# Row sums of attention's squares, five attention units later in TensorE's order

## The chip, the cores and the metric

The kernel runs on one NeuronCore of a Trainium2 chip. Its engines are named as in the profile: PE (TensorE, matrix multiplication; PEld is its weight load), DVE (VectorE), ACT (ScalarE), POOL (GpSimd) and SP (SyncE, which issues DMAs). Each engine executes its own queue in order, and waits on semaphores for the others. The metric is the device time of one execution in microseconds (us), lower is better.

## The reference

One decoder layer on 2048 tokens of width 1024, in float32. A normalised input is projected once; the columns go to two groups of heads, whose outputs are normalised, put side by side and projected again. A SwiGLU feed-forward part and a gated per-layer embedding follow.

```python
u = rmsnorm(h, attn_pre_norm[i])
proj = u @ w_in[i]
hq, hf, hi, hg, sq, sk, sv = jnp.split(proj, splits, axis=-1)
o_hg = hgrn2_mix(hq, hf, hi, lb_all[i])                        # 4 heads, gated linear recurrence
o_hg = rmsnorm(o_hg.astype(x.dtype), hg_out_norm[i]) * jax.nn.silu(hg)
o_sb = stick_breaking_mix(sq.reshape(B, T, SB_HEADS, SB_DH), ...)  # 8 heads of width 64, causal
o_sb = rmsnorm(o_sb, sb_out_norm[i])
mix = jnp.concatenate([o_hg, o_sb], axis=-1) @ w_out[i]
h = h + rmsnorm(mix, attn_post_norm[i])
u = rmsnorm(h, ffn_pre_norm[i])
gate, up = jnp.split(u @ w_gate_up[i], [D_FF], axis=-1)
y = (jax.nn.silu(gate) * up) @ w_down[i]
h = h + rmsnorm(y, ffn_post_norm[i])
h = h + (p[i] @ ple_proj[i]) * jax.nn.sigmoid(h @ ple_gate[i])
```

The line that matters here is `o_sb = rmsnorm(o_sb, ...)`: it needs, for each token, the sum of the squares of all 512 attention outputs.

## The kernel before

The 2048 tokens are four groups (0 to 3) of 512. A float32 product is made of three: each operand is split into a high part (ACT casts it, "wh", "uh", "ah") and a low part (DVE or POOL subtracts, "wl", "ul", "al"), and `mm3`, lines 216 to 218, multiplies high by high and the two mixed pairs. Weights come by DMA into one of four "wr" buffers and are split in `weight` (L202 on ACT, L203 on DVE and POOL in turn).

Attention is a stream of units (`attention`, L404). For a group g, a head h and a chunk c of 512 keys, a unit is one block of 128: `weights_of` makes the scores on PE (two matmuls into "z", L429), two sigmoids on ACT (L435, L436), a scan on DVE (L450) and the weights "a" on POOL (L454). Four units later (LAG), `turn_of` transposes the blocks of "a" on PE into the bank "tr" (L462, up to four transposes), ACT copies it out as the high part "ah" (L465) and DVE subtracts the low part "al" (L467). One unit later still, `values_of` multiplies both parts by the values into the bank "av" (L478 and L479). PSUM has eight banks: three "mm", two "z", and one each of "av", "tr" and "hg".

When a head is through, ACT and DVE bring its result to SBUF (L486, L487). After every second head, ACT squares the pair's result (L490), POOL adds the square to the tile "sbacc" (L492), and `result` splits it (L291 on ACT, L292 on DVE) and stores it (L293, L294). After the last head of a group four matmuls by a column of ones sum the squares over the partitions into four columns of "tr" (L497; in float32 each shows as two passes), and ACT copies them to "oss" (L498). The output projection of that group scales by them: POOL makes "rg" of "oss" (L655, L656).

The order of PE is the order in which the program is written (`manual_schedule` for PE alone); the other engines' orders are made by a scheduler from the dependencies and its own estimates, so they follow when PE's order changes. What PE does between the units comes from `weave`: it steps a main stream (an input projection of a group; after the last of these the output projections of groups 0 and 1) and the side streams (attention, HGRN2, operands of later stages) in a fixed rhythm. So attention of groups 0 to 2 ends in the middle of a projection, with the next group's units right behind, and that of group 3 ends with the output projection of group 1, "the second output projection". The third one (group 2) follows at once. HGRN2 has its own row sums (L639) in the bank "hg".

Of the kernel before, what the change touches and what calls it, by code (L numbers as in the profile page):

```python
# [8 lines left out]
F32 = mybir.dt.float32  # L9
# [6 lines left out]
P = 128  # L16
# [3 lines left out]
GT = 512  # L20
NG = T // GT
TT = GT // P
HH = 4
SBH = 8
# [66 lines left out]
def hybrid_block(  # L91
# [6 lines left out]
    nc = tc.nc  # L98
# [44 lines left out]
    ones1 = ctile("ones1", (P, 1))  # L143
# [15 lines left out]
    oss = ctile("oss", (P, NG, 2 * TT))  # L159
# [6 lines left out]
    def bank(tag):  # L166
        return ps.tile([P, 512], F32, tag=tag, name=tag, bufs=BANKS[tag])
# [19 lines left out]
    att = side.enter_context(tc.tile_pool(name="att", bufs=2, side="right"))  # L187
# [213 lines left out]
                yield  # L401


    def attention():  # L404
        def head_start(g, h):
            st = {"g": g, "h": h}
            st["q"] = []
            for i in range(2):
                t = att.tile([P, GT], F32R, tag=f"q{i}", name=f"q{i}")
                for half in range(2):  # L410
                    nc.sync.dma_start(t[half * SBD:(half + 1) * SBD, :].bitcast(F32), q_s[g][i, h])
                st["q"].append(t)
            return st

        def chunk_start(st, c):
            h = st["h"]
            kt = att.tile([P, GT], F32R, tag="kt", name="kt", bufs=2)
            nc.sync.dma_start(kt.bitcast(F32), k_s[c][h].rearrange("i d t -> (i d) t"))
            vt = att.tile([P, TT, P], F32R, tag="vt", name="vt", bufs=2)
            nc.sync.dma_start(vt.bitcast(F32), v_s[c][:, h, :].rearrange("(b s) d -> s b d", s=P))  # L420
            return {"st": st, "c": c, "k": kt, "v": vt, "a": []}

        def weights_of(ch, tb):
            st, c = ch["st"], ch["c"]
            diag = c == st["g"]
            n = (tb + 1) * P if diag else GT
            z = bank("z")
            for i in range(2):
                nc.tensor.matmul(  # L429
                    z[:, :n], st["q"][i][:, tb * P:(tb + 1) * P], ch["k"][:, :n],  # L430
                    start=i == 0, stop=i == 1)
            if diag:
                nc.vector.tensor_tensor(z[:, n - P:n], z[:, n - P:n], maskneg, op=ALU.add)  # L433
            be = att.tile([P, GT], F32, tag="be", name="be")
            nc.scalar.activation(be[:, :n], z[:, :n], AF.Sigmoid, scale=0.125)  # L435
            nc.scalar.activation(z[:, :n], z[:, :n], AF.Sigmoid, scale=-0.125)  # L436


            r, j = ring[tb], st["g"] - c
            o = GT if j % 2 == 0 else 0  # L440
            if diag:
                init = 1.0
                if c > 1:
                    nc.gpsimd.memset(r[:, o + n:o + n + 1], 1.0)
            elif j % 2 == 0:
                init = r[:, 0:1]
                nc.scalar.copy(r[:, 2 * GT:2 * GT + 1], init)
            else:
                init = r[:, GT:GT + 1]
            nc.vector.tensor_tensor_scan(  # L450
                r[:, o:o + n][:, ::-1], z[:, :n][:, ::-1], be[:, :n][:, ::-1], init,
                op0=ALU.mult, op1=ALU.bypass)
            a = att.tile([P, GT], F32, tag="a", name="a", bufs=8)
            nc.gpsimd.tensor_tensor(a[:, :n], be[:, :n], r[:, o + 1:o + n + 1], op=ALU.mult)  # L454
            ch["a"].append(a)

        def turn_of(ch, sb):
            diag = ch["c"] == ch["st"]["g"]
            t0 = sb if diag else 0
            tr = bank("tr")  # L460
            for tb in range(t0, TT):
                nc.tensor.transpose(tr[:, tb * P:(tb + 1) * P], ch["a"][tb][:, sb * P:(sb + 1) * P], ident)  # L462
            lo_c = t0 * P
            hi = att.tile([P, GT], F32R, tag="ah", name="ah")
            nc.scalar.copy(hi[:, lo_c:], tr[:, lo_c:])  # L465
            lo = att.tile([P, GT], F32R, tag="al", name="al")
            nc.vector.tensor_tensor(lo[:, lo_c:], tr[:, lo_c:], hi[:, lo_c:].bitcast(F32), op=ALU.subtract)  # L467
            return ch, sb, lo_c, hi, lo

        def values_of(ch, sb, lo_c, hi, lo):  # L470
            st, c = ch["st"], ch["c"]
            g = st["g"]
            first = c == g and sb == 0
            last = c == 0 and sb == TT - 1
            if first:
                st["av"] = bank("av")
            av = st["av"]
            nc.tensor.matmul(av[:, lo_c:], ch["v"][:, sb, :], hi[:, lo_c:], start=first, stop=False)  # L478
            nc.tensor.matmul(av[:, lo_c:], ch["v"][:, sb, :], lo[:, lo_c:], start=False, stop=last)  # L479
            if last:  # L480
                h = st["h"]
                mine, other = slice(h % 2 * SBD, (h % 2 + 1) * SBD), slice((1 - h % 2) * SBD, (2 - h % 2) * SBD)
                if h % 2 == 0:
                    avo[0] = att.tile([P, GT], F32, tag="avo", name="avo", bufs=1)
                o = avo[0]
                nc.scalar.copy(o[mine, :], av[other, :])  # L486
                nc.vector.tensor_tensor(o[mine, :], av[mine, :], o[mine, :], op=ALU.add)  # L487
                if h % 2:
                    sq = sb_acc if h == 1 else att.tile([P, GT], F32, tag="be", name="sq")
                    nc.scalar.activation(sq, o, AF.Square)  # L490
                    if h > 1:
                        nc.gpsimd.tensor_tensor(sb_acc, sb_acc, sq, op=ALU.add)  # L492
                    result(g, HH + h // 2, o, g_sb[:, h // 2:h // 2 + 1], nc.vector)
                    if h == SBH - 1:
                        b = bank("tr")
                        for t in range(TT):
                            nc.tensor.matmul(b[:, t:t + 1], sb_acc[:, t * P:(t + 1) * P], ones1, start=True, stop=True)  # L497
                        nc.scalar.copy(oss[:, g, TT:], b[:, 0:TT])  # L498

        sb_acc = att.tile([P, GT], F32, tag="sbacc", name="sbacc", bufs=1)  # L500
        avo = [None]
        units, turned = [], []
        chunks = [(g, h, c) for g in range(NG) for h in range(SBH) for c in range(g, -1, -1)]
        n_units = len(chunks) * TT
        for i in range(n_units + LAG + 1):
            if i < n_units:
                if i % TT == 0:
                    g, h, c = chunks[i // TT]
                    if c == g:
                        st = head_start(g, h)  # L510
                    ch = chunk_start(st, c)
                weights_of(ch, i % TT)
                units.append((ch, i % TT))
            yield
            if turned:
                values_of(*turned.pop(0))
            if i >= LAG and i - LAG < n_units:
                turned.append(turn_of(*units[i - LAG]))
            yield

    LAG = 4
# [739 lines left out]
    for g in range(NG - 1):  # L1261
        if g + 1 < NG - 1:
            out_load(g + 1, res[g + 1])
        op = Stream(out_proj(g, res[g]))
        if g == 0:
            weave(op, 2, rates.part(2), r2.part(2))
            hgs[2].drain()
            weave(op, OP_SLOTS - 2, rates.part(OP_SLOTS - 2), r3.part(OP_SLOTS - 2))
        elif g == 1:
            weave(op, half, rates.part(half), r3.part(half), (pm, TT, 0))  # L1270
            tu = Stream(turn(un_s[0], u_s[0], g_ffn, ["mm"], xt, ev))
            weave(op, half, rates.part(half), r3.part(half), (tu, 9, 0))
            hgs[3].drain()
            att_stream.drain()
            side.close()
            big[0] = ctx.enter_context(tc.tile_pool(name="bigr", bufs=1, side="right"))
            mm_tags[:] = ["mm", "z", "mm", "z", "mm", "av"]
        else:
            out_load(NG - 1, res[NG - 1])
            weave(op, half, (pm, TT, 0))  # L1280
            weave(op, half, (Stream(first_operands()), ND, 1))
        op.drain()
        pm = Stream(post_mix(g, res[g]["mix"]))
# [4 lines left out]
    op = Stream(out_proj(NG - 1, res[NG - 1]))  # L1288
# [42 lines left out]
    for g in range(NG):  # L1331
        stage, step, every, lag, tag = (
            (1, 67, 2, 3, "mm"), (2, 0, 1, 2, "hg"), (3, 67, 2, 3, "mm"), (4, 0, 1, 4, "hg"))[g]
# [35 lines left out]
```

## Time and profile before

| what | value |
|---|---|
| median of 3 runs | 3015.01 us (3011.72 to 3019.57) |
| the profiled execution's own time | 3018.84 us |
| its span, first to last instruction | 3017.1 us |
| mean granted clock of TensorE | 0.990 |
| busy: PE / DVE / ACT / POOL | 2906.5 / 2066.9 / 1581.6 / 1403.9 us |
| row sums L497 on PE | 32 passes, 212.1 to 1356.3 us |
| POOL's addition L492 | 12 times, median 1.293 us each |
| ACT's square L490 | 16 times, about 0.63 us each |

In a row of the timeline the first number is the start and the second the busy time, both in us; then the engine, the line, the operation, what is written and read, its shape and how many instructions are merged. A bracket gives the idle time of the engine just before and the instruction whose end released it. In a row of waits the three numbers are the sum, how often, and the longest. Ends of matmuls are modelled; starts are the better measure of pace. A few records are missing from the trace.

### The profile page before, as it was taken

Reading aid. Unit: us, or ns where it says so; the run is one execution under the profiler, and the core shown is the slowest. Engines: PE = TensorE matmul, PEld = TensorE weight load, DVE = VectorE, ACT = ScalarE, POOL = GpSimd, SP = SyncE. Lnnn points to the kernel's source line nnn. Section 1 sums busy time; section 2 is a strip of 40 time slices with the busy share of each in tenths; the row PEclk is TensorE's granted clock in tenths of the full one; section 3 lists DMA queues with packets and bytes.
Section 4 is the critical chain, followed back from the end, with each engine's and each line's share of the span. In section 5 each row is a group of like instructions: output and inputs, shape, how many; then the busy total and the mean of one; then the engine's idle time right before and its main releaser. Section 6 shows DMA issues by size and latency. Waiting matters only on the chain. (4 is left out here: it accounts for less than half of the span.)

```text
span 3017.1 us, 52727 instructions
## 1 busy us (share of the span) xinstructions
PE 2906.5 (96%) x18188; PEld 2427.5 (80%) x18188; DVE 2066.9 (69%) x2985; ACT 1581.6 (52%) x3186; POOL 1403.9 (47%) x1396
## 2 busy tenths in 40 slices
PE   9999999999999999888899999999999999999999
PEld 7788787878788788788878788888788888878777
DVE  3566676787677777764787777655777765666785
ACT  5666766677666766665633333455433233545442
POOL 3344555655566575754533221355722121456653
PEclk9999999999999999999999999999999999999999
DMA  7765564555546446567877677667965555667974
GB/s 227 214 201 172 176 185 149 159 174 168 152 133 207 134 151 187 195 227 252 289 227 252 215 262 251 216 201 221 331 199 171 174 168 174 208 221 232 324 246 160
DMA packets 478379, 619.05 MB, mean 205 GB/s; under 512 B 43936, under 2 KB 278432, under 8 KB 478112
## 3 DMA queue, kind: packets, MB, share of 16 engines
q1 hardware_dynamic: 478112, 615.69, 64.6%
q8 instruction: 143, 2.34, 0.3%
q14 instruction: 124, 1.02, 0.1%
HBM read 448.28 MB, written 167.25 MB: 204 GB/s over the span
## 5 line engine op out<-in xcount | busy, mean ns | idle before, releaser
L819 ACT CAST wh<-wr 128x512 fp32r<-128x512 f32 x600 | 351.4, 617 | 464.9 <-PE mm L217 191.3
L820 POOL TENSOR_TENSOR wl<-wr,wh 128x512 fp32r<-128x512 f32 x256 | 372.3, 1460 | 463.9 <-ACT wh L819 432.7
L454 POOL TENSOR_TENSOR a<-be,ring 128x512 f32<-128x512 f32 (+2 forms) x320 | 319.8, 1000 | 422.9 <-DVE ring L450 399.7
L216 PE MATMUL mm<-uh,wh 128*128 128x512 f32 x1168 | 481.5, 412 | 5.0 <-DVE vv L369 1.7
L217 PE MATMUL mm<-ul,wh 128*128 128x512 f32 x1168 | 461.0, 395 | 3.8 <-DVE ul L820 3.4
L218 PE MATMUL mm<-uh,wl 128*128 128x512 f32 x1168 | 461.9, 395 | 1.2 <-DVE wl L820 1.2
L820 DVE TENSOR_TENSOR wl<-wr,wh 128x512 fp32r<-128x512 f32 x344 | 296.8, 869 | 174.7 <-ACT wh L819 146.7
L450 DVE TENSOR_TENSOR_SCAN ring<-z,ring,be 128x512 f32<-128x512 f32 x192 | 245.6, 1279 | 100.6 <-ACT z L436 95.8
L216 PE MATMUL mm<-wh,uh 128*128 128x256 f32 (+1 forms) x992 | 307.5, 310 | 0.4 <-DVE vv L369 0.4
L217 PE MATMUL mm<-wl,uh 128*128 128x256 f32 (+1 forms) x992 | 293.3, 296 | 1.8 <-POOL wl L820 1.8
L218 PE MATMUL mm<-wh,ul 128*128 128x256 f32 (+1 forms) x992 | 293.2, 296 | 0.0
L218 PEld LDWEIGHTS mm<-uh,wl 128*128 128x128 f32 x1168 | 220.7, 189 | 52.1 <-DVE wl L820 1.6
L216 PEld LDWEIGHTS mm<-uh,wh 128*128 128x128 f32 x1168 | 222.0, 190 | 49.9 <-DVE ul L338 2.0
L217 PEld LDWEIGHTS mm<-ul,wh 128*128 128x128 f32 x1168 | 221.9, 190 | 45.0 <-DVE ul L820 3.9
L202 ACT CAST wh<-wr 128x512 fp32r<-128x512 f32 x288 | 178.5, 620 | 128.2 <-PE mm L217 70.5
L203 POOL TENSOR_TENSOR wl<-wr,wh 128x512 fp32r<-128x512 f32 x144 | 190.6, 1323 | 112.4 <-ACT wh L202 109.6
L467 DVE TENSOR_TENSOR al<-tr,ah 128x512 fp32r<-128x512 f32 (+1 forms) x320 | 191.8, 599 | 69.4 <-ACT ah L465 66.8
L435 ACT ACTIVATE be<-z 128x512 f32<-128x512 f32 (+2 forms) x320 | 171.0, 534 | 111.6 <-DVE z L433 61.8
L465 ACT CAST ah<-tr 128x512 fp32r<-128x512 f32 (+1 forms) x320 | 167.7, 524 | 91.6 <-PE tr L462 89.6
L820 POOL TENSOR_TENSOR wl<-s,wh 128x512 fp32r<-128x512 f32 x44 | 67.7, 1541 | 291.8 <-ACT wh L819 274.1
L216 PEld LDWEIGHTS mm<-wh,uh 128*128 128x128 f32 x992 | 191.2, 193 | 8.5 <-issue 0.6
L217 PEld LDWEIGHTS mm<-wl,uh 128*128 128x128 f32 x992 | 191.7, 193 | 7.5 <-POOL wl L820 2.2
(314 smaller groups left out, 7189.9 us busy)
## 6 DMA issues: line engine op xcount, KB each, us to landing
wr<-in_w_gate_up_dram SPq DMA_DIRECT2D x308, 256.0 KB, 4.0
wr<-in_w_in_dram SPq DMA_DIRECT2D x224, 256.0 KB, 3.2
wr<-hid_s SPq DMA_DIRECT2D x154, 256.0 KB, 3.2
wr<-in_w_down_dram SPq DMA_DIRECT2D x110, 256.0 KB, 3.3
wr<-wd_s SPq DMA_DIRECT2D x88, 256.0 KB, 3.1
kt<-k_s SPq DMA_DIRECT2D x80, 256.0 KB, 3.3
vt<-v_s SPq DMA_DIRECT2D x80, 256.0 KB, 3.2
wr<-h_s SPq DMA_DIRECT2D x80, 256.0 KB, 4.5
```

Of the source, the lines that this page charges most:

```text
L202: nc.scalar.copy(hi, src)
L203: (lo_engine or nc.gpsimd).tensor_tensor(lo, src, hi.bitcast(F32), op=ALU.subtract)
L216: nc.tensor.matmul(o, l[0], r[0], start=start, stop=False)
L217: nc.tensor.matmul(o, l[0], r[1], start=False, stop=False)
L218: nc.tensor.matmul(o, l[1], r[0], start=False, stop=stop)
L435: nc.scalar.activation(be[:, :n], z[:, :n], AF.Sigmoid, scale=0.125)
L450: nc.vector.tensor_tensor_scan(r[:, o:o + n][:, ::-1], z[:, :n][:, ::-1], be[:, :n][:, ::-1], init, op0=ALU.mult, op1=ALU.bypass)
L454: nc.gpsimd.tensor_tensor(a[:, :n], be[:, :n], r[:, o + 1:o + n + 1], op=ALU.mult)
L465: nc.scalar.copy(hi[:, lo_c:], tr[:, lo_c:])
L467: nc.vector.tensor_tensor(lo[:, lo_c:], tr[:, lo_c:], hi[:, lo_c:].bitcast(F32), op=ALU.subtract)
L819: nc.scalar.copy(hi, src)
L820: lo_engine.tensor_tensor(lo, src, hi.bitcast(F32), op=ALU.subtract)
```

## The change

The four row-sum matmuls and the copy behind them become a function, `row_sums(g)`. For groups 0, 1 and 2 the end of the group's last head only notes that a sum is due; a counter lets four further units pass, and in the step after that the sums are issued behind that step's value product and transposes. For group 3 they are issued after the second output projection has been drained. Nothing else is added or left out. Line numbers behind the function are higher by 8 to 14 in the changed file.

```diff
+    def row_sums(g):
+        b = bank("tr")
+        for t in range(TT):
+            nc.tensor.matmul(b[:, t:t + 1], sb_acc[:, t * P:(t + 1) * P], ones1, start=True, stop=True)
+        nc.scalar.copy(oss[:, g, TT:], b[:, 0:TT])
...
                     result(g, HH + h // 2, o, g_sb[:, h // 2:h // 2 + 1], nc.vector)
-                    if h == SBH - 1:
-                        b = bank("tr")
-                        for t in range(TT):
-                            nc.tensor.matmul(b[:, t:t + 1], sb_acc[:, t * P:(t + 1) * P], ones1, start=True, stop=True)
-                        nc.scalar.copy(oss[:, g, TT:], b[:, 0:TT])
+                    if h == SBH - 1 and g < NG - 1:
+                        sums_due.append((TT, g))
...
             if i >= LAG and i - LAG < n_units:
                 turned.append(turn_of(*units[i - LAG]))
+            if sums_due:
+                n, g = sums_due.pop()
+                if n:
+                    sums_due.append((n - 1, g))
+                else:
+                    row_sums(g)
             yield
...
             hgs[3].drain()
             att_stream.drain()
+            op.drain()
+            row_sums(NG - 1)
             side.close()
```

On PE, at the end of group 0, the order before was:

```order
L429 MATMUL z<-kt,q_2623 128x512
L429 MATMUL z<-kt,q_2626 128x512
L478 MATMUL av<-ah,vt 128x128
L479 MATMUL av<-al,vt 128x128
L497 MATMUL tr<-ones_193,sbacc 128x1 x4
L462 MATMUL tr<-ident,a 128x128 x4
L216 MATMUL mm<-uh,wh 128x512
L217 MATMUL mm<-ul,wh 128x512
```

There the transposes now follow the value product directly, and the sums (now L409) stand four units further on, behind the next transposes (now L470):

```order
L437 MATMUL z<-kt,q_2922 128x128
L437 MATMUL z<-kt,q_2925 128x128
L486 MATMUL av<-ah,vt 128x128
L487 MATMUL av<-al,vt 128x128
L470 MATMUL tr<-ident,a 128x128 x4
L409 MATMUL tr<-ones_193,sbacc 128x1 x4
L216 MATMUL mm<-uh,wh 128x512
L217 MATMUL mm<-ul,wh 128x512
```

The sums moved past 57 rows of PE's queue; they and the transposes ahead of them write the one bank "tr". Groups 1 and 2 have the same pattern, with HGRN2's small matmuls or a score pair behind the sums in place of the six matmuls.

ACT's order at the end of group 1 shows what the scheduler makes of it. Before:

```order
L486 COPY avo<-av 64x512
L490 ACTIVATE sq<-avo 128x512
L291 ACTIVATE oh<-avo,g_sb 128x512
L498 COPY oss<-tr 128x4
L465 CAST ah<-tr 128x512
L435 ACTIVATE be<-z 128x512
```

And with the change (L494 is the copy of the result, L473 the operand copy, L498 the square, L410 the small copy):

```order
L494 COPY avo<-av 64x512
L473 CAST ah<-tr 128x512
L498 ACTIVATE sq<-avo 128x512
L291 ACTIVATE oh<-avo,g_sb 128x512
L443 ACTIVATE be<-z 128x512
...
L473 CAST ah<-tr 128x512
L410 COPY oss<-tr 128x4
L202 CAST wh<-wr 128x512
```

The operand copy of the next transposes moved ahead of the square, and the small copy stands behind the operand copy of the transposes after which the sums are issued.

On POOL, behind the end of attention in group 3, the order before was:

```order
L706 TENSOR_TENSOR h<-h,mix 128x512
L655 TENSOR_SCALAR rg<-oss 128x8
L268 TENSOR_SCALAR ssum<-ss 128x1
L656 TENSOR_TENSOR rg<-rg,neghalf 128x8
L271 TENSOR_TENSOR rstd_18398<-ssum,neghalf 128x1
L268 TENSOR_SCALAR ssum<-ss 128x1
L271 TENSOR_TENSOR rstd_18479<-ssum,neghalf 128x1
L706 TENSOR_TENSOR h<-h,mix 128x512
L203 TENSOR_TENSOR wl<-wr,wh 128x512
```

And with the change (L665 and L666 are the scale "rg", L716 the addition "h"):

```order
L665 TENSOR_SCALAR rg<-oss 128x8
L666 TENSOR_TENSOR rg<-rg,neghalf 128x8
L716 TENSOR_TENSOR h<-h,mix 128x512
L268 TENSOR_SCALAR ssum<-ss 128x1
L271 TENSOR_TENSOR rstd_18398<-ssum,neghalf 128x1
L268 TENSOR_SCALAR ssum<-ss 128x1
L271 TENSOR_TENSOR rstd_18479<-ssum,neghalf 128x1
L203 TENSOR_TENSOR wl<-wr,wh 128x512
L716 TENSOR_TENSOR h<-h,mix 128x512
```

The scale of the third projection moved ahead of the first addition, and the weight's low half (L203) ahead of the second.

More of the change, by code (lines that the diff above doesn't have):

```diff
@@ L401, in in_proj @@
                 yield
+    sb_acc = att.tile([P, GT], F32, tag="sbacc", name="sbacc", bufs=1)
+    def row_sums(g):
[3 more added lines that the diff above has]
+        nc.scalar.copy(oss[:, g, TT:], b[:, 0:TT])
     def attention():
@@ L493, in values_of @@
                     result(g, HH + h // 2, o, g_sb[:, h // 2:h // 2 + 1], nc.vector)
-                    if h == SBH - 1:
-                        b = bank("tr")
-                        for t in range(TT):
-                            nc.tensor.matmul(b[:, t:t + 1], sb_acc[:, t * P:(t + 1) * P], ones1, start=True, stop=True)
-                        nc.scalar.copy(oss[:, g, TT:], b[:, 0:TT])
-        sb_acc = att.tile([P, GT], F32, tag="sbacc", name="sbacc", bufs=1)
-        avo = [None]
+                    if h == SBH - 1 and g < NG - 1:
+                        sums_due.append((TT, g))
+        avo, sums_due = [None], []
         units, turned = [], []
```

## The prediction

> **What bounds the kernel now.** I read the page's busy shares first, then the list of waits for TensorE alone, then the timeline around the longest of them.
>
> ```profile
> span 3017.1 us, 52727 instructions
> PE 2906.5 (96%) x18188; PEld 2427.5 (80%) x18188; DVE 2066.9 (69%) x2985; ACT 1581.6 (52%) x3186; POOL 1403.9 (47%) x1396
> ...
> PE tr L497 <- POOL sbacc L492: 19.0, 4, 5.2
> PE av L479 <- DVE al L467: 18.0, 30, 3.4
> PE z L217 <- POOL wl L203: 9.1, 5, 3.4
> ```
>
> TensorE is busy for 96% of the span, so what it idles is nearly all that an order alone can win. The columns of the waits are the sum, the number of times and the longest. The first of them belongs to the instruction that the change moves: four times TensorE stands before the row sums (L497) until POOL has added the last square (L492), 19.0 us in all. The first of the four places, at the end of group 0, shows why, and what the idle time drags behind it:
>
> ```profile
> 206.17 1.09 POOL L454 TENSOR_TENSOR a<-be,ring 128x512 f32<-128x512 f32 x1 [2.15 <-DVE ring L450]
> 206.66 0.27 PE L479 MATMUL av<-al,vt 128*128 128x128 f32 x1
> 209.29 0.69 DVE L487 TENSOR_TENSOR avo<-av,avo 64x512 f32<-64x512 f32 x1
> 210.07 0.63 ACT L490 ACTIVATE sq<-avo 128x512 f32<-128x512 f32 x1 [1.53 <-DVE avo L487]
> 210.78 1.26 POOL L492 TENSOR_TENSOR sbacc<-sbacc,sq 128x512 f32<-128x512 f32 x1 [0.36 <-ACT sq L490]
> 212.10 1.87 PE L497 MATMUL tr<-ones,sbacc 128*128 128x1 f32 x8 [5.17 <-POOL sbacc L492]
> 219.23 0.40 PE L478 MATMUL av<-ah,vt 128*128 128x512 f32 x1
> ...
> 210.00:212.00 2.00, 0.00 (x0) 0.54 0.32 111
> 216.00:218.00 2.00, 2.00 (x8) 0.76 0.00 0
> ```
>
> The last value product ends at 206.93 (206.66 + 0.27); add, square and sum then run one after another on DVE, ACT and POOL until 212.04. The last two rows are windows of TensorE (length, busy time with its count, granted clock, DMA share, GB/s). With half clock as the only other state, 0.54 puts the fall at 210.2 and 0.76 the return at 217.0: 6.8 us at half clock. So a stall costs more than its 5.17 us of waiting; the sums and most of the work up to 217 run at half speed.
>
> **The change part by part.** What TensorE does in place of waiting follows already in its order: transposes (L462), six matmuls (L216 to L218), the pair of scores (L429). Their full-clock pace, with the twin of the row sums (HGRN2's, L639):
>
> ```profile
> 467.47 0.60 PE L462 MATMUL tr<-ident,a 128*128 128x128 f32 x4
> 467.82 0.47 PE L216 MATMUL mm<-uh,wh 128*128 128x512 f32 x1
> 469.30 0.63 PE L429 MATMUL z<-kt,q 128*128 128x512 f32 x2
> ...
> 1346.41 0.95 PE L639 MATMUL hg<-ones,acc 128*128 128x1 f32 x8
> ```
>
> From start to start four transposes take 0.35 us (467.82 - 467.47) and six matmuls 1.48 (469.30 - 467.82). I count 0.63 for a score pair, its whole duration, and 0.95 for the eight row-sum passes, against 1.87 at half clock.
>
> *Removed, groups 0 to 2.* I measure from the end of the last value product to the next one (L478), which closes the stretch. Group 0: 219.23 - 206.93 = 12.30 us. Without the sums the same work waits first for POOL's weights "a" (206.17 + 1.09 = 207.26) and then needs 0.35 + 1.48 + 0.63 + 1.48 = 3.94: it ends at 211.2, a gain of 8.0. Its own inputs are there by then: ACT's order now has the operand copy (L465) right behind the copy of the result (L486), and DVE, free of L487 at 209.98, needs one more step of about that length, 0.7 us, so 210.7. The two others:
>
> ```profile
> 471.97 0.40 PE L479 MATMUL av<-al,vt 128*128 128x512 f32 x1
> 483.62 0.39 PE L478 MATMUL av<-ah,vt 128*128 128x512 f32 x1
> 817.23 0.40 PE L479 MATMUL av<-al,vt 128*128 128x512 f32 x1
> 828.29 0.40 PE L478 MATMUL av<-ah,vt 128*128 128x512 f32 x1
> ```
>
> Group 1: 483.62 - 472.37 = 11.25, against 0.35 + 0.63 + 1.48 = 2.46; gain 8.8. Group 2: 828.29 - 817.63 = 10.66, against the same and HGRN2's small matmuls (L559), which I count as one more pair, 0.63, so 3.09; gain 7.6. Together **24.4 us**.
>
> *What is late next.* ACT, DVE and POOL still have the end of the head to do (L486, L487, L490, L291, L292, L492), now while TensorE goes on. The ends of the other odd heads show what that costs, since they do the same without row sums. At one of them:
>
> ```profile
> 330.93 0.44 PE L479 MATMUL av<-al,vt 128*128 128x384 f32 x1 [0.89 <-DVE al L467]
> ```
>
> The next value product but one waited 0.89 us for DVE's low half. I take 0.9 at each place, **-2.7 us**; the bounds are 0, if the head's end fits in beside, and 1.2, if ACT also evicts a bank first (a third more, an estimate).
>
> *Added, groups 0 to 2: a new wait.* The sums use the bank "tr", of which there is one, and in the new order they stand directly behind four transposes into that bank. They cannot start before ACT and DVE have read these transposes out (L465, then L467). At the new places the kernel before shows how long that takes:
>
> ```profile
> 229.24 0.33 PE L462 MATMUL tr<-ident,a 128*128 128x128 f32 x1 [0.31 <-POOL a L454]
> 230.28 0.69 DVE L467 TENSOR_TENSOR al<-tr,ah 128x512 fp32r<-128x512 f32 x1 [0.22 <-ACT ah L465]
> 493.64 0.62 PE L462 MATMUL tr<-ident,a 128*128 128x128 f32 x4
> 495.60 0.68 DVE L467 TENSOR_TENSOR al<-tr,ah 128x512 fp32r<-128x512 f32 x1
> 838.96 0.62 PE L462 MATMUL tr<-ident,a 128*128 128x128 f32 x4
> 840.29 0.69 DVE L467 TENSOR_TENSOR al<-tr,ah 128x512 fp32r<-128x512 f32 x1
> ```
>
> Group 0: TensorE would be free at about 229.3 (the fourth transpose, a quarter of 0.35) and DVE ends at 230.97: 1.7 us. Group 1: free at 494.0, DVE ends at 496.28, which is 2.3; in the new order DVE does this ahead of two HGRN2 steps (L562, L598) that stood before it, so I take 1.8, next to the others. Group 2: 839.3 to 840.98: 1.7. Behind the waiting sums stand six matmuls or a score pair on TensorE; on ACT the small copy to "oss" waits for the sums, with a cast or the next probabilities (L435) behind it. With the sums themselves, 3 x 0.95, this is **-8.05 us**. Bounds: at the least 3 x (1.4 + 0.95) = 7.05, if the two reads, of about 0.7 us each, start at once; at the most 3 x (2.5 + 1.7 + 0.95) = 15.5, if each wait grows to 2.5 us and halves the clock for half as long as the 6.8 us above, which loses 1.7 us.
>
> Whether 1.7 us lowers the clock is read from other waits:
>
> ```profile
> 1299.64 0.49 PE L623 MATMUL hg<-score,v 128*128 128x128 f32 x2 [1.88 <-DVE sl L619]
> 1299.00:1303.00 4.00, 3.36 (x29) 1.00 0.23 80
> 1369.79 0.39 PE L217 MATMUL z<-wl,uh 128*128 128x256 f32 x1 [2.56 <-POOL wl L203]
> 1371.00:1374.00 3.00, 3.00 (x16) 0.50 1.05 402
> ```
>
> After 1.88 us it stayed at 1.00; after 2.56 us it fell to 0.50. I take it as kept. [...]
>
> *Group 3.* Here the sums move behind the last 12 matmuls of the second output projection, not behind transposes:
>
> ```profile
> L202 ACT CAST wh<-wr 128x512 fp32r<-128x512 f32 x288 | 178.5, 620 | 128.2 <-PE mm L217 70.5
> ...
> 1347.62 0.36 PE L216 MATMUL mm<-wh,uh 128*128 128x256 f32 x1
> 1349.36 0.40 PE L479 MATMUL av<-al,vt 128*128 128x512 f32 x1
> 1354.81 0.37 PE L497 MATMUL tr<-ones,sbacc 128*128 128x1 f32 x1 [5.05 <-POOL sbacc L492]
> 1359.24 0.41 PE L216 MATMUL z<-wh,uh 128*128 128x256 f32 x1
> 1366.40 1.65 POOL L706 TENSOR_TENSOR h<-h,mix 128x512 f32<-128x512 f32 x1 [1.53 <-DVE mix L705]
> 1368.02 1.71 POOL L203 TENSOR_TENSOR wl<-wr,wh 128x512 fp32r<-128x512 f32 x1
> ```
>
> Twelve such matmuls and one value product took 1349.36 - 1347.62 = 1.74 us, so TensorE stands again from 1351.5 at the latest (1349.76 + 1.74). ACT's new order puts one weight cast (0.62) ahead of the square, so the sums start at 1355.4, still at half clock, and need 1.87: the third projection starts at 1357.3 instead of 1359.24, 1.9 us sooner. That lead meets the wait at 1369.79 for a weight's low half, which POOL starts at 1368.02 behind a residual addition (L706). In the new order this weight stands ahead of that L706, 1.65 us, so the wait gives way by about as much as the lead. Bounds: -3 (a slow power, L656, now stands ahead of the first L706, and two weight loads on SP behind the stores of "oh" and "avo"; about two steps of 1.65 lost) to +7 (the lead, the 2.56 us of wait, and some of the half clock behind it all go). I take **+3 us**, near to the lead and a part of that wait.
>
> *Sum.* 24.4 - 2.7 - 8.05 + 3 = 16.65, so about 17 us less. The profiled execution took 3018.84 us (its span and 1.7 around it), which gives 3001.8; it lies 3.8 above the median of the runs, 3015.0, against which I forecast **2998 us**.
>
> **The rivals.** *The new wait eats the gain.* ACT and DVE, behind with the head's end, read the transposes late; each new wait is 2.5 us and halves the clock. For it: the margin between 1.88 and 2.56 is small, and group 1 has up to 2.3. Against it: the new places lie some 17 us behind the old ones, when the backlog is worked off. With nothing won in group 3: 24.4 - 2.7 - 15.5 = 6.2 less, about 3009 us, not to be told from no change (0.3%, 9 us, is about what a measurement of this kernel can tell).
>
> *Group 3 gives its part back.* POOL holds the third projection, the lead is lost there, and 3 us more: 24.4 - 2.7 - 8.05 - 3 = 10.65 less, 3004 us. For it: five waits for weights' low halves, 9.1 us, are that stage's. Against it: the weight moves ahead in POOL's order.
>
> *Slower: the blocked ACT queue.* The small copy holds ACT from its own read of the transposes until the sums are done, about 0.7 + 0.95 = 1.7 us, with scores, scan and weights behind it. If that backlog stopped TensorE by over (16.65 + 9) / 3 = 8.6 us at each of the three places, the kernel would take 3024 us or more. Against it: ACT is busy for 52% of the span, so 1.7 us are made up in some 4 us.
>
> *The change does nothing.* Only if the sum of squares were late at the new place too; in group 0 it ends at 212.04 and the place is at 229.3. Excluded for groups 0 to 2; in group 3 it is what I count.
>
> **How the numbers follow.** Forecast 0.70; new wait 0.13; group 3 gives back 0.12; slower 0.05. Faster by over 0.3%: 0.70 + 0.12 = 0.82; within 0.3%: 0.13; slower: 0.05. The range: the good bounds together give 24.4 - 0 - 7.05 + 7 = 24.4 less, 2990.6, so 2990 us; the upper end takes in the new wait with a little kept, 3008 us.
>
> **What would show it.** The waits for "sbacc" should be one of about 4 us in place of four; three new waits of 1.7 to 1.8 us for DVE's "al" should stand before the sums; their eight passes should take about 0.95 us; the clock should stay at 1.00 at the three old and the three new places. It is wrong if the new waits exceed 2.3 us with half clock behind them, or if the waits of L479 for "al", 18.0 us now, grow by more than 4 us.

## The result, and the profile after

The changed kernel takes 3005.56 us (median of 9 runs, 3001.98 to 3016.13) against 3019.46 us for the kernel before beside it (9 runs, 3011.72 to 3027.7). The ratio is 0.9962, with a 95% interval of 0.9945 to 0.9978, so 0.38% of 3019.46, or 11.5 us, are gained (6.6 to 16.6); the two medians lie 13.9 us apart. A repetition (5 runs, below) gave 0.9966 (0.9954 to 0.9978). The forecast was 17 us and 2998 us: the sign and the range held, and the gain by the ratio was about a third smaller.

The page's span and busy shares after, and the list of waits for TensorE (sum, times, longest), show the exchange that was expected:

```profile
span 3000.7 us, 52727 instructions
PE 2899.6 (97%) x18188; PEld 2418.7 (81%) x18188; DVE 2074.1 (69%) x2985; ACT 1580.2 (53%) x3186; POOL 1407.2 (47%) x1396
...
PE av L487 <- DVE al L475: 20.4, 33, 3.4
PE z L217 <- POOL wl L203: 6.6, 6, 1.7
...
PE tr L409 <- DVE al L475: 4.4, 3, 1.5
PE tr L409 <- POOL sbacc L500: 4.3, 1, 4.3
```

The four waits for "sbacc" (19.0 us) have become one of 4.3; three waits of 1.5 us for the operand's low half stand before the sums in their new place; the waits of the value product for "al" grew from 18.0 to 20.4 and those for a weight's low half shrank from 9.1 to 6.6.

TensorE's timeline at group 0 follows, first at the old place of the sums, then at the new one, and last its windows (length, busy time with its count, granted clock, DMA share, GB/s):

```profile
206.15 0.27 PE L487 MATMUL av<-al,vt 128*128 128x128 f32 x1
210.21 0.40 PE L486 MATMUL av<-ah,vt 128*128 128x512 f32 x1
213.24 0.44 PE L486 MATMUL av<-ah,vt 128*128 128x384 f32 x1 [0.22 <-ACT ah L473]
214.43 0.44 PE L487 MATMUL av<-al,vt 128*128 128x384 f32 x1 [0.75 <-DVE al L475]
...
222.54 1.05 PE L409 MATMUL tr<-ones,sbacc 128*128 128x1 f32 x8 [1.46 <-DVE al L475]
223.46 0.48 PE L216 MATMUL mm<-uh,wh 128*128 128x512 f32 x1
...
224.81 0.63 PE L217 MATMUL mm<-ul,wh 128*128 128x512 f32 x1
...
210.00:214.00 4.00, 3.46 (x16) 1.00 0.66 229
222.00:224.00 2.00, 1.46 (x10) 1.00 1.09 277
224.00:226.00 2.00, 2.00 (x7) 0.52 0.16 49
226.00:228.00 2.00, 2.00 (x8) 0.63 0.04 8
```

At the old place TensorE now goes on, from the last value product (ends 206.42) to the next one (210.21) in 3.79 us instead of 12.30, and the clock stays at 1.00. At the new place the wait is 1.46 us and the eight passes 0.92 (223.46 - 222.54). But behind them, with TensorE busy all the time, the clock is 0.52 and then 0.63: a matmul of 512 columns takes 0.63 us in place of 0.40. The same views at groups 1 and 2:

```profile
468.11 0.40 PE L487 MATMUL av<-al,vt 128*128 128x512 f32 x1
470.64 0.39 PE L486 MATMUL av<-ah,vt 128*128 128x512 f32 x1
471.19 0.51 PE L487 MATMUL av<-al,vt 128*128 128x512 f32 x1 [0.15 <-DVE al L475]
475.61 0.44 PE L487 MATMUL av<-al,vt 128*128 128x384 f32 x1 [0.99 <-DVE al L475]
484.40 1.05 PE L409 MATMUL tr<-ones,sbacc 128*128 128x1 f32 x8 [1.46 <-DVE al L475]
...
810.04 0.39 PE L487 MATMUL av<-al,vt 128*128 128x512 f32 x1
813.15 0.40 PE L486 MATMUL av<-ah,vt 128*128 128x512 f32 x1
816.95 0.44 PE L486 MATMUL av<-ah,vt 128*128 128x384 f32 x1 [0.98 <-ACT ah L473]
818.31 0.44 PE L487 MATMUL av<-al,vt 128*128 128x384 f32 x1 [0.92 <-DVE al L475]
827.88 1.05 PE L409 MATMUL tr<-ones,sbacc 128*128 128x1 f32 x8 [1.46 <-DVE al L475]
...
486.00:488.00 2.00, 2.00 (x7) 0.73 0.00 0
488.00:490.00 2.00, 2.00 (x9) 0.50 0.04 6
490.00:492.00 2.00, 2.00 (x10) 0.92 0.44 125
828.00:830.00 2.00, 2.00 (x13) 1.00 0.47 145
```

Group 1 repeats group 0, half clock behind the sums included. Group 2 has the same wait and the same sums, and the clock stays.

As one measure of groups 0 to 2 together I take ACT's squares: from the last one of group 0 (210.07 before) to the last one of group 3. Between them lie all three exchanges and nothing of group 3's. The rows that are still needed, first of the kernel before, then of the kernel after, with TensorE's sums and the third projection's start of group 3:

```profile
1352.78 0.63 ACT L490 ACTIVATE sq<-avo 128x512 f32<-128x512 f32 x1
```

```profile
209.57 0.63 ACT L498 ACTIVATE sq<-avo 128x512 f32<-128x512 f32 x1 [0.41 <-DVE avo L495]
...
1342.79 0.63 ACT L498 ACTIVATE sq<-avo 128x512 f32<-128x512 f32 x1
...
1344.97 1.87 PE L409 MATMUL tr<-ones,sbacc 128*128 128x1 f32 x8 [4.26 <-POOL sbacc L500]
1346.69 0.56 PE L216 MATMUL z<-wh,uh 128*128 128x256 f32 x1
```

The stretch was 1352.78 - 210.07 = 1142.7 us and is 1342.79 - 209.57 = 1133.2: 9.5 us less, where the prediction's sum for the three groups was 24.4 - 2.7 - 8.05 = 13.65. In group 3 the third projection starts 3.90 us after the last square (1346.69 - 1342.79), before 6.46 (1359.24 - 1352.78): a lead of 2.6 us.

### The profile page after: what moved, and what is told of

Read it like the earlier page. It is cut to its first block, busy times and chain, and to the rows that moved or that the text cites. A ratio compares the mean times of both kernels' runs of the same rounds, so it can differ in the third digit from the quotient of the medians.

```text
span 3000.7 us, 52727 instructions
## 1 busy us (share of the span) xinstructions
PE 2899.6 (97%) x18188; PEld 2418.7 (81%) x18188; DVE 2074.1 (69%) x2985; ACT 1580.2 (53%) x3186; POOL 1407.2 (47%) x1396
## 4 chain that ended last, share of the span: by engine, by line
PE 45%; DMA 5%; DVE 4%; POOL 3%; issue 2%; ACT 1%; SPq 0%; POOLq 0%; DVEq 0%; ACTq 0%
PE mm L216 6%; PE mm L217 6%; PE mm L218 6%; PE z L217 4%; PE z L218 4%; PE z L216 4%; PE av L217 2%; PE av L216 2%; PE av L218 2%; PE tr L217 2%; PE tr L216 2%; PE tr L218 2%; DMA wr<-in_w_gate_up_dram 1%; DMA wr<-u_s 1%; DMA wr<-h_s 1%
## 5 line engine op out<-in xcount | busy, mean ns | idle before, releaser
L203 POOL TENSOR_TENSOR wl<-wr,wh 128x512 fp32r<-128x512 f32 x144 | 190.0, 1320 | 114.0 <-ACT wh L202 109.9
L473 ACT CAST ah<-tr 128x512 fp32r<-128x512 f32 (+1 forms) x320 | 167.6, 524 | 89.4 <-PE tr L470 87.2
```

The costliest lines, as they stand in the source:

```text
L203: (lo_engine or nc.gpsimd).tensor_tensor(lo, src, hi.bitcast(F32), op=ALU.subtract)
```

## The experiments

Two questions stood open: why the clock fell behind waits of 1.46 us, when it had stayed after 1.88 us in the kernel before, and whether group 3 adds anything. My theory for the first was the order within the step: the sums stand behind the transposes, hence the wait; and after the wait come passes that move a single column each, which keep TensorE "busy" in the profile but may not hold the clock up. The rivals were the wait alone, and the busy time spent on the sums whatever it consists of. All edits are against the changed kernel. The table gives the stretch defined above, from one profiled execution each. "Transposes ahead of the sums", "all out of the way" and "the change again" ran on another chip than the other four.

| kernel | median us (runs) | ratio to before, 95% | stretch, us |
|---|---|---|---|
| before | see above | 1 | 1142.7 |
| the change | 3005.56 (9) | 0.9962 (0.9945 to 0.9978) | 1133.2 |
| the change again | 3005.26 (5) | 0.9966 (0.9954 to 0.9978) | 1134.8 |
| sums ahead of the transposes | 3001.3 (4) | 0.9939 (0.9916 to 0.9962) | 1128.8 |
| groups 0 to 2 only | 3010.13 (10) | 0.9974 (0.9963 to 0.9986) | 1133.5 |
| group 3 only | 3019.38 (10) | 1.0001 (0.9991 to 1.0011) | 1147.3 |
| sums four times | 3014.09 (1) | | 1145.7 |
| transposes ahead of the sums | 3008.57 (1) | | 1138.0 |
| all out of the way | 2992.7 (6) | 0.9931 (0.9916 to 0.9946) | 1128.6 |

With group 3 only, the stretch has the order of the kernel before, and still took 4.6 us longer; 3.4 us of that are clock, 34.1 us of the stretch being at half clock in place of 27.3. So one execution's stretch is good to about that, and differences below it are read from the timelines and the runs, not from this column.

**Sums ahead of the transposes.** In groups 0 to 2 the sums go ahead of that step's transposes, not behind them.

```diff
             if turned:
                 values_of(*turned.pop(0))
-            if i >= LAG and i - LAG < n_units:
-                turned.append(turn_of(*units[i - LAG]))
             if sums_due:
                 ...
                     row_sums(g)
+            if i >= LAG and i - LAG < n_units:
+                turned.append(turn_of(*units[i - LAG]))
             yield
```

> The row sums of groups 0 to 2 are issued four units later as in the change, but ahead of that step's transposes instead of behind them, when the bank tr is free; group 3 as in the change. Theory (the added wait is the bank's, and the half clock behind it comes from that wait together with the one-column passes): the three waits of 1.46 us for al before the sums vanish, the transposes wait some 0.3 us for the small copy as in the kernel before, the clock stays at 1.00 at the three new places; about 3 x 1.2 + 2.8 = 6 us less than with the change, so about 20 us less than before. Rival (the read-out of the bank is due anyway, so the wait only moves to the next value product): 0 to 2 us less than with the change.

TensorE's timeline of this kernel at group 0's sums, and its window there, then a row and a window at the end of group 2's head:

```profile
222.66 1.00 PE L409 MATMUL tr<-ones,sbacc 128*128 128x1 f32 x8
223.92 0.66 PE L470 MATMUL tr<-ident,a 128*128 128x128 f32 x4 [0.25 <-ACT oss L410]
...
222.00:224.00 2.00, 1.75 (x15) 1.00 1.03 246
...
815.94 0.63 PE L218 MATMUL mm<-uh,wl 128*128 128x512 f32 x1
...
816.00:818.00 2.00, 2.00 (x6) 0.50 0.00 0
```

The sums wait for nothing, in all three groups; what is left is 0.25 us that the transposes wait until ACT has copied the sums. The clock stays at 1.00 at all three new places (222 to 228, 482 to 488 and 822 to 828). So the 1.46 us were the price of one bank written by two steps one behind the other, and not of the sums. In this execution one half-clock window turned up elsewhere, at 816, behind the two waits of nearly 1 us at the head's end in group 2. The change has these waits too, there without loss; the sums four times (at 824.5) and the last version (at 811.9) lose the clock behind them again. No single-column pass stands there. The stretch is 4.4 us shorter than with the change; the intervals of the two ratios overlap, so the runs alone don't prove this kernel faster than the change.

**Groups 0 to 2 only.** Group 3's sums stay at the end of its last head.

```diff
-                    if h == SBH - 1 and g < NG - 1:
-                        sums_due.append((TT, g))
+                    if h == SBH - 1:
+                        if g < NG - 1:
+                            sums_due.append((TT, g))
+                        else:
+                            row_sums(g)
...
             op.drain()
-            row_sums(NG - 1)
             side.close()
```

> Only the sums of groups 0 to 2 are moved, as in the change; group 3's stand where they stood before. Theory (each of the three places gives about 3.4 us): the square at 939.5 us in the kernel before starts some 10.4 us sooner, and nothing more is won from there to 1458 us; 10 us less than before, plus or minus some 4 us of clock windows later on. Rival (most of the gain is group 3's): under 5 us less.

The ratio of 0.9974 makes 7.8 us of 3018.29. Wait and half clock at groups 0 and 1 are there again (half clock from 226.6 to 230.0 and from 489.5 to 492.9), and again not at group 2 (1.00 from 826 to 838).

**Group 3 only.** Groups 0 to 2 have their sums at the old place.

```diff
                     if h == SBH - 1 and g < NG - 1:
-                        sums_due.append((TT, g))
+                        row_sums(g)
```

> Only the sums of group 3 are moved behind the second output projection; those of groups 0 to 2 stand where they stood before. Theory: the wait for sbacc there falls from 5.05 to about 4.3 us, the third projection starts some 2 us sooner and its waits for low halves shrink, so that by 1458 us about 4.5 us are won: 3 to 6 us less than before. Rival (POOL holds that projection and takes the lead back): no change, 0 to 1 us.

The ratio is 1.0001 (0.9991 to 1.0011): at most 2.7 us gained. So groups 0 to 2 alone give nearly all that can be told: 7.8 and -0.3 add up to 7.5, the change gave 11.5 and, in the repetition, 10.3. Each lies within the others' intervals. A part of 2 or 3 us for group 3 is neither shown nor excluded. The trace does show a lead at first: from the last square to the start of the last residual addition ("h" on POOL) it takes 1450.14 - 1359.18 = 91.0 us, before 1447.61 - 1352.78 = 94.8. But executions with the new place of group 3's sums range from 90.4 (the change) to 94.9 (sums four times), and groups 0 to 2 only, with the old place, has 93.8.

**Sums four times.** This and the next kernel put extra work on TensorE at the new places, without any wait, to part "busy" from "working". Both have the sums ahead of the transposes. Here each row-sum matmul of groups 0 to 2 is done four times over (the result is the same), 32 passes of one column.

```diff
+        for again in range(4 if g < NG - 1 else 1):
-        for t in range(TT):
-            nc.tensor.matmul(b[:, t:t + 1], sb_acc[:, t * P:(t + 1) * P], ones1, start=True, stop=True)
+            for t in range(TT):
+                nc.tensor.matmul(b[:, t:t + 1], sb_acc[:, t * P:(t + 1) * P], ones1, start=True, stop=True)
```

> As e1_sums_first, but the four row-sum matmuls of groups 0 to 2 are issued four times over into the same columns (32 passes, some 3.8 us at full clock); the output stays the same. Theory (passes with one moving column hardly count as work for the clock): the clock falls to one half at two or three of the three places though TensorE waits for nothing before them. Rival (only waiting lowers the clock, and the two falls with the change were the waits' own, by where the windows happened to lie): the clock stays at 1.00 at all three.

TensorE's timeline and windows, at the three places one after another:

```profile
220.76 4.15 PE L410 MATMUL tr<-ones,sbacc 128*128 128x1 f32 x32
...
222.00:224.00 2.00, 2.00 (x19) 0.95 1.01 266
224.00:226.00 2.00, 1.75 (x10) 0.50 0.52 158
226.00:228.00 2.00, 2.00 (x7) 0.50 0.05 8
...
485.81 3.68 PE L410 MATMUL tr<-ones,sbacc 128*128 128x1 f32 x32
...
490.00:492.00 2.00, 2.00 (x38) 0.51 0.03 8
...
832.15 4.52 PE L410 MATMUL tr<-ones,sbacc 128*128 128x1 f32 x32
...
836.00:838.00 2.00, 1.75 (x9) 0.50 0.00 1
```

**Transposes ahead of the sums.** In place of the 24 extra passes, 28 transposes of the identity go into the same bank, and the sums once behind them. The transposes' results are overwritten or not read.

```diff
     def row_sums(g):
         b = bank("tr")
+        for again in range(7 if g < NG - 1 else 0):
+            for t in range(TT):
+                nc.tensor.transpose(b[:, t * P:(t + 1) * P], ident, ident)
         for t in range(TT):
```

> As e1_sums_first, but 28 transposes of the identity into the same bank stand ahead of the four row-sum matmuls of groups 0 to 2 and are overwritten by them; this control takes about as long as the 32 passes of e4_sums_four_times (28 x 0.1 + 0.95 = some 3.8 us), with matmuls of 128 columns in place of one. Theory (what lowers the clock is that the array has almost nothing to do in a one-column pass): the clock stays at 1.00 behind all three places. Rival (any such stretch of small, separate matmuls lowers it): it falls at two or three of them, as in e4_sums_four_times.

The same views at group 0:

```profile
222.91 3.25 PE L410 MATMUL tr<-ident 128*128 128x128 f32 x28
225.99 0.95 PE L412 MATMUL tr<-ones,sbacc 128*128 128x1 f32 x8
...
222.00:224.00 2.00, 2.00 (x17) 1.00 0.88 267
224.00:226.00 2.00, 2.00 (x21) 1.00 1.01 277
226.00:228.00 2.00, 1.75 (x16) 1.00 0.41 128
```

This pair answers a part of the first question. Both kernels keep TensorE busy for about 4 us at each place, without a wait ahead of it, with nearly the same number of instructions. With single columns the clock fell to half at all three places; with 128 columns ahead of the sums it fell at none (at 490 and 833 the windows show 1.00 too). Neither a wait nor the busy time explains that. In these two runs the clock did not go by the busy share of the profile (1.75 to 2.00 of every 2 us in the windows above): a row-sum pass takes as long as a transpose (3.68 / 32 = 0.115 us against (225.99 - 222.91) / 28 = 0.110), and yet 32 of the one halved the clock where 28 of the other, with 8 passes behind them, left it at 1.00. My reading is that a row-sum pass counted little or not at all here; in the change, 1.46 us of waiting and 0.92 us of such passes would then make 2.4 us without work, an estimate from the rows of group 0. The eight passes without the wait did not lower the clock, at three of three places in the first experiment. That the wait alone would not have done it is argued, not shown: no run has this wait with ordinary matmuls behind it.

How long a wait may be cannot be read from one execution. The wait of 1.88 us after which the clock had stayed in the kernel before (HGRN2's, for "sl") is in every trace, 1.88 to 1.91 us long and with the same matmuls behind it. In the change, its repetition and groups 0 to 2 only the clock stayed there too; in the other five it fell. The first experiment's row and window:

```profile
1285.96 0.49 PE L633 MATMUL hg<-score,v 128*128 128x128 f32 x2 [1.91 <-DVE sl L629]
...
1287.00:1288.00 1.00, 1.00 (x7) 0.50 0.46 174
```

The record of clock changes that each trace keeps shows what differs. In the kernel before and in the change it has two values, 1.00 and 0.50. Six stretches at half clock last 3.41 us and six last 6.83 in the kernel before, six and two in the change, not counting the last stretch of each, which ends with the execution. Every stretch at full clock between them lasts a whole multiple of 3.41 us (3 to 250 times in the kernel before). Two more traces show the same lengths (3.4 us from 226.6 in groups 0 to 2 only, 6.8 from 223.8 in the sums four times). So within each of these executions the changes lie on a grid, and where the grid lies differs: a boundary at 1299.0 in the kernel before and one at 1286.90 in the first experiment are 3.5 of its steps apart. In the five executions that lost the clock, the whole wait lies in one piece of the grid (the first experiment: wait 1284.05 to 1285.96, piece 1283.49 to 1286.90). In the four others a boundary cuts it, with 1.1 to 1.7 us in the larger part (the kernel before: 1297.76 to 1299.64, cut at 1299.0; the change: 1287.33 to 1289.23, cut at 1289.0). That is what nine executions show; that it holds beyond them is not shown.

The grid fits group 2 too, where the same 2.4 us cost nothing: in all three executions with the sums behind the transposes a boundary cuts them there and leaves at most 1.8 us in one piece (the change: 826.42 to 828.79, cut at 828.2), against 1.9 to 2.4 us at groups 0 and 1. With 1.8 against 1.9 us this is near the edge, so for group 2 it is a fit and no proof.

**All out of the way.** The sums of groups 0 to 2 go ahead of the transposes, and group 3's go into the middle of the third output projection, where "sbacc" is long complete. For that the tile lives in a pool that stays open.

```diff
-    sb_acc = att.tile([P, GT], F32, tag="sbacc", name="sbacc", bufs=1)
+    sb_acc = wpool.tile([P, GT], F32, tag="sbacc", name="sbacc", bufs=1)
...
             op.drain()
-            row_sums(NG - 1)
             side.close()
...
             weave(op, half, (pm, TT, 0))
+            row_sums(NG - 1)
             weave(op, half, (Stream(first_operands()), ND, 1))
```

(with the edit of the first experiment)

> As e1_sums_first, and the sums of group 3 stand in the middle of the third output projection in place of ahead of it (the tile sbacc lies in a pool that is still open there). Theory (group 3's place still holds 4.3 us of waiting and a half-clock stretch): no row sum waits anywhere for sbacc, the clock stays at 1.00 there, and the third projection ends 3 to 6 us sooner than in e1_sums_first; in all 22 to 26 us less than before, about 2994 us. Rival (POOL and ACT hold that projection, so the lead is lost at the waits for weights that follow): as e1_sums_first within 1 us.

TensorE's timeline at group 3's sums:

```profile
1362.93 0.95 PE L409 MATMUL tr<-ones,sbacc 128*128 128x1 f32 x8
1363.74 0.36 PE L216 MATMUL z<-wh,uh 128*128 128x256 f32 x1
```

No sum waits any more, and the eight passes of group 3 take 0.95 us in place of 1.87. The clock, expected to stay at 1.00 in that stage, still falls there: at 1358.0, ahead of the sums, behind a wait of 2.14 us for a weight's low half; the matmuls of 256 columns take 0.41 us in place of 0.28 until 1361.3. The kernel is the best of all: 0.9931 (0.9916 to 0.9946) against 0.9966 (0.9954 to 0.9978) of the change on the same chip, beside the same runs of the kernel before. The intervals don't touch. How much of the step comes from group 3's place and how much from the order of the sums was not parted by runs. In the traces, from the last square to the start of the last residual addition, it is 88.2 us here and 90.9 in the first experiment; that 2.7 us is less than this measure differs between executions with group 3's sums at one place (90.4 to 94.9).

**The change again.** The changed kernel unaltered, on the chip of the last one.

> The change itself once more, on the same chip as e6_all_out_of_the_way, for a direct comparison: 11 to 17 us less than before. If the gain of its group 3 part is lost later on, as e3_group_3 leaves open, nearer to 8.

3005.26 us, ratio 0.9966: 10.3 us less, which lies between the two values expected and decides nothing about group 3. Its trace has the half clock behind the sums of groups 0 and 1 again (0.78 and 0.50 from 224 to 228, 0.50 and 0.66 from 488 to 492). So it is no accident of one execution.

## Why the prediction was right, and where it was wrong

Point by point, with its own terms:

- *What bounds the kernel, and the sign.* Right. Three of four stalls are gone, and what TensorE idles was worth what the prediction said.
- *Removed, 24.4 us.* Measured in the same way: 12.30 - (210.21 - 206.42) = 8.5, then 11.25 - (470.64 - 468.51) = 9.1, then 10.66 - (813.15 - 810.43) = 7.9; together 25.5. The clock at the old places stayed at 1.00.
- *What is late next, -2.7 us.* The mechanism was right and the size too small: the rows show two waits at each place, 0.22 + 0.75, 0.15 + 0.99, 0.98 + 0.92, together 4.0 us. I had taken one wait for a low half alone. In groups 0 and 2 one for the high half came on top, which ACT wrote behind its part of the head's end (L498, L291) and other work; in group 1 a second one for a low half.
- *The new wait, 1.7 to 1.8 us, and the sums, 0.95.* Right in kind, a little too dear: 3 x (1.46 + 0.92) = 7.1 in place of 8.05.
- *"I take it as kept", the clock.* This step of the prediction failed. The clock fell behind two of the three sums. By the windows that is (1 - 0.52) x 2 + (1 - 0.63) x 2 = 1.7 us in group 0, and 0.54 + 1.0 + 0.16 = 1.7 in group 1: 3.4 us that the sum had at nothing. Two things were wrong. I read the bounds, 1.88 kept and 2.56 lost, from one execution, and the wait of 1.88 loses the clock in five of nine. And I compared the new wait with waits behind which full matmuls came, and left out that here eight single-column passes follow; 32 of them halved the clock without any wait at three of three places (sums four times). Whether the wait alone would have lowered the clock stays open. The rival "the new wait eats the gain" had the half clock, but asked for waits of 2.5 us for it; it came at 1.46.
- *Groups 0 to 2 together.* 25.5 - 4.0 - 7.1 - 3.4 = 11.0, against 13.65 predicted; the squares show 9.5. The remaining 1.5 us I cannot assign; it is within what one execution's stretch is good for.
- *Group 3, +3 us.* The wait of 4.26 us and the start of the third projection came as worked out (a lead of 2.6 us at the start, predicted 1.9), and the waits for weights' low halves fell by 2.5 us, from 9.1 to 6.6. But done alone the move gave nothing that 10 runs can tell (at most 2.7 us). The term stays open, and the rival "group 3 gives its part back" with it.
- *The blocked ACT queue.* ACT did stand for the sums, 1.87 us ahead of its small copy at group 0, and no stall of 8.6 us followed. That rival is excluded. So is "the change does nothing".
- *The two signs of being wrong.* New waits above 2.3 us with half clock behind: the waits were shorter, and the half clock came all the same, so that sign was set up wrongly. The waits for "al" grew by 2.4, below the 4 that I had named.

The forecast of 2998 us was 7.6 us too low against the median. The three groups lack 13.65 - 9.5 = 4.2 us of the sum, most of it the half clock. The profiled executions differ by 3017.1 - 3000.7 = 16.4 us, nearly the 16.65 of the sum, but that is luck: the three groups gave 9.5 of it in place of 13.65, and the rest 6.9 in place of 3. The medians of the runs differ by less; a single execution of this kernel is not measured to better than some us.

## What to carry to other kernels

When a step is put off to fill a stall, look at what stands directly ahead of it in the buffer it writes: behind the transposes it inherited a wait of 1.46 us, ahead of them 0.25. And when you judge whether a wait will cost the clock, I would add the passes of a single column beside it to the wait: here 32 of them alone, 3.7 to 4.5 us with TensorE busy throughout, halved the clock at three of three places. Whether a given wait costs it, read from several executions, not from one: the 1.9 us before HGRN2's "sl" did so in five of nine. Where a consumer is far off, put the step where its input is long complete, in the middle of other matmuls; the version that did this, with the sums ahead of the transposes, beat both kernels.

## What the runs showed of the hardware

I had not expected that a TensorE which the profile shows as busy without a gap can lose its clock: 32 passes of one column (3.7 to 4.5 us) halved it at three of three places, 28 transposes of 128 columns and 8 such passes in about the same time at none. Nor that the same wait, with the same matmuls around it, costs the clock in one execution and not in another: 1.9 us did so in five of nine, each time when the wait lay whole in one piece of a grid of 3.41 us. The same 1.46 us of waiting and the same sums cost it at groups 0 and 1 and not at group 2, in all three executions. Where the half-clock stretches fall differs between executions, and by an estimate this is part of why runs of one kernel differ: with groups 0 to 2 only, the fastest and the slowest run (3002.86 and 3016.58 us, 13.7 apart) have a mean clock of 0.993 and 0.988, and 0.005 x 3010 is 15 us.
